# Two scan directions in lockstep, and one layer's modulation multiplied on TensorE

## The chip, the cores and the metric

The kernel runs on one core of one Trainium2 chip. The metric is the device time of one execution in microseconds (us). Engines: PE is TensorE (matrix products), DVE VectorE, ACT ScalarE, POOL GpSimd, SP SyncE, which issues nearly all DMAs here. SBUF holds the operands, PSUM (eight banks) the results of TensorE. An fp32 matmul counts as two instructions in the trace ("passes" below), and each has a weight load (PEld) that overlaps others.

## What is computed

A two-layer backbone over 1024 latent tokens and 256 context tokens of width 1024. Layer 0 mixes tokens by an RWKV-7 recurrence in both directions, layer 1 by a 2-D Fourier transform; each is followed by a squared-ReLU MLP. The part that matters is the recurrence, 16 heads of 64 channels, and the modulation vectors:

```
def step(s, inp):                       # s: one 64 x 64 state per head
    w_t, k_t, v_t, a_t, b_t = inp[:5]
    sa = jnp.einsum('bhvk,bhk->bhv', s, a_t)
    s = s * w_t[:, :, None, :] + sa[..., None] * b_t[:, :, None, :] + v_t[..., None] * k_t[:, :, None, :]
    y = jnp.einsum('bhvk,bhk->bhv', s, inp[5]) if with_out else None
...
for d in range(N_DIRS):                 # d = 1 runs from the end
    yc, s_ctx = _wkv_scan(st_c.get('r'), vh_c, *st_c['dirs'][d], s0, rev)
    yl, _ = _wkv_scan(st_l['r'], vh_l, *st_l['dirs'][d], s_ctx, rev)
...
sh1, sc1, ga1, sh2, sc2, ga2 = jnp.split((silu_c @ mod_w[i] + mod_b[i])[:, None, :], N_MOD, axis=-1)
```

`mod_w[i]` is 1024 x 6144; of layer 0's six vectors the last four (4096 columns) are wanted only behind the scan.

## The kernel before

Three stages follow each other, with some overlap: the projections (`p1_plan`, to about 640 us) write the scan's factors to DRAM, `scan` runs the recurrence (640 to 1315 us), and `rest` does the readout, the MLPs and the Fourier layer.

**The scan.** 1280 tokens are cut into 20 chunks of 64; `scan_step(i)` does chunk i of both directions, d = 0 and d = 1. Within a chunk the recurrence is solved by matrices. For each direction: products of B^T with the factors, `mms` (L945), whose results ScalarE and VectorE mask and copy out (L954 to L966); a transposition of the factor tile bk on TensorE (`trs`, L975) and its copy (L979). `scan_invert` inverts the triangular 32 x 32 blocks of both directions and all heads at once, with VectorE (L1094 to L1138), two products h (L1145) and t (L1156) and a copy tt. None of that needs the state. Then comes what does: VectorE multiplies the old state t by the decay `pcs` into the tile sv, once for each half of the partitions (L1001), GpSimd does the same into st (L1004). The product x (L1019) fills four 32-row quarters of one bank B: two of block row 0 (z = 0) and two of block row 1. For z = 0: ScalarE copies x to xs (L1026), u multiplies by the inverse (L1031), two copies bring u to sv (L1036), o subtracts the coupling from B's other half (L1044); for z = 1: copy, u, two copies. At the end s (L1056) gives the new state and y (L1072, L1076) the output. u and o of one direction use two of the array's four groups of 32 rows. The head halves hh = 0, 1 lie on partitions 0 to 63 and 64 to 127.

**The modulation of layer 0 inside the scan.** The host lays `k_mwt` out transposed: 32 blocks of 128 output columns, the inner dimension along the free axis in two halves. In each of steps 3 to 18 four blocks of 256 KB are loaded into the ring mw (W0 to W3), each released by the step's last x (`after=[self.at]`), and VectorE multiplies each with a row of SiLU(c) and sums it (`mod_part`, L886). `silu_row` makes the row twice, at steps 3 and 11. Layer 1's modulation goes the same way later, beside the first MLP (`modvecs`).

**The order.** `Plan.add` only records an operation: engine (q is SyncE's queue), booked duration, keys read and written, and load (how much of the array the clock is booked to see). `Plan.flex` leaves the engine open. `Plan.emit` then writes out the order of every engine's queue, by booked times alone: always the operation that can start first, and among equals the one with the longest booked path to the end. On the chip each engine runs its queue in that order and waits where an operand is late. In idle time of TensorE the planner may put fill products (L1814) that keep the clock up. PSUM banks and places in SBUF are taken as they are booked free. The scan uses banks 0 to 3 for `mms` and transposes, 4 for h and t, 5 to 7 for x, u, s and y.

Of the kernel before, what the change touches and what calls it, by code (L numbers as in the profile page):

```python
# [13 lines left out]
ALU = mybir.AluOpType  # L14
# [66 lines left out]
class Plan:  # L81
# [245 lines left out]
class Kernel:  # L327
# [449 lines left out]
    def factor(self, kt, low, d, c, k, k_k, kk, kkk, rr):  # L777
# [37 lines left out]
        self.flex_tt(n, bk[:, :ng, 0], gv(ta), p1[:, :ng], ALU.mult, [kta, kp1], [(kbk, 0)])  # L815
# [19 lines left out]
    def scan(self):  # L835
# [10 lines left out]
        for j, hp in enumerate(R["hp"]):  # L846
            plan.add("dve", 0.6, lambda hp=hp: nc.vector.tensor_copy(hp, self.cst[:, 0:32].rearrange("p (e c) -> p e c", e=1).broadcast_to(
                [P, 16, 32])), [self.kcst], [("hp", j)])
        self.state = {}
        for i in range(NCH):  # L850
            self.plan.step = i
            self.scan_step(i)
            if i == 3:
                past = plan.gate([("indt", 0), ("rts", 0), ("rts", 1)])
# [25 lines left out]
    def mod_part(self, layer, j, h, w, kw, after=()):  # L880

        nc = self.nc
        row = (j - 16 if layer == 0 else 32 + j) * P
        src = self.i["k_mwt"][row : row + P, h * 512 : h * 512 + 512]
# [15 lines left out]
    def scan_step(self, i):  # L900
# [3 lines left out]
        R0 = [slice(hh * 64, hh * 64 + 32) for hh in range(2)]  # L904
        R1 = [slice(hh * 64 + 32, hh * 64 + 64) for hh in range(2)]
# [24 lines left out]
        for d in range(2):  # L930
# [5 lines left out]
            for h4 in range(2):  # L936
# [13 lines left out]
                for hh, B in enumerate(BB):  # L950
# [3 lines left out]
                    plan.add("act", 0.38, lambda B=B, hh=hh, ys=ys: nc.scalar.activation(  # L954
                        mab[R0[hh], :, ys].rearrange("p w q t -> p q w t"),
                        B.tile[R0[hh]].rearrange("p (q w t) -> p q w t", q=4, w=4)[:, :, 0:2], AF.Copy, scale=-0.5),
                        [B], [(kM, d, hh, h4, 0)], B)
                    plan.add("act", 0.28, lambda bv=bv, hh=hh, ys=ys: nc.scalar.activation(
                        mab[R1[hh], 0, ys], bv()[R1[hh], :, 32:C], AF.Copy, scale=-0.5),
# [10 lines left out]
            BB = [self.plan.bank(range(4)) for _ in range(2)]  # L970

            def trs(BB=BB, bk=bk):
                for q in range(8):
                    for hh, rs in enumerate(HR):
                        nc.tensor.transpose(BB[hh].tile[:, q * C : (q + 1) * C], bk[rs, q, :], self.ident[rs, rs])  # L975

            plan.add("pe", 1.1, trs, [kb], [*BB, (kt_, 0), (kt_, 1)], load=0.5)
            for hh, B in enumerate(BB):
                plan.add("act", 0.68, lambda B=B, bkt=bkt, hh=hh: nc.scalar.activation(  # L979
                    bkt[:, hh].rearrange("p x t -> p (x t)"), B.tile, AF.Copy, scale=self.sgn[:, hh : hh + 1]),  # L980
                    [B, self.ksgn], [(kt_, hh)], B)
        tt, kT = self.scan_invert(mab, kM)

        for d in range(2):
# [941 lines left out]
```

## Time and profile before

| | us |
|---|---|
| median of 3 runs (lowest, highest) | 3095.93 (3091.98, 3108.24) |
| the profiled execution | 3100.86 |
| its span, first to last instruction | 3099.1 |
| TensorE busy in it | 2905.6 |
| VectorE, ScalarE, GpSimd busy | 1902.2, 998.6, 535.9 |
| mean granted clock of TensorE | 0.93 of full |

Busy times are sums over one profiled execution on the one core. Matmuls are pipelined and their ends are modelled, so a busy TensorE is not one at its peak. [...] In names of tiles the first letter is the stage (a, b projections, s scan, r rest) and the rest the place; ps is PSUM. "Chain of waits" is the chain of work that ended last, followed back from the last instruction; a DMA's piece in it runs from its issue to its landing.

### The profile page before, as it was taken

What the parts mean: (1) busy time and instruction counts of PE and PEld (TensorE: products, weight loads), DVE (VectorE), ACT (ScalarE), POOL (GpSimd) and SP (SyncE); (2) the same over time, 40 slices, a digit from 0 to 9 for tenths busy, and PEclk for the clock granted to TensorE, in tenths of its full rate; (3) what the DMA queues carried; (4) which work ended last, traced back from release to release, by engine and by line L of the source; (5) the groups of instructions that cost most, each with busy time, mean ns of one, the idle gap of its engine ahead of it and who ended that gap; (6) DMA issues with size and microseconds to landing.
All of it is one profiled execution on the core that took longest, in us unless ns stands there. A gap on an engine that the chain in (4) does not pass through costs nothing.

```text
span 3099.1 us, 65486 instructions
## 1 busy us (share of the span) xinstructions
PE 2905.6 (94%) x27884; PEld 2258.6 (73%) x27884; DVE 1902.2 (61%) x3316; ACT 998.6 (32%) x1943; POOL 535.9 (17%) x449
## 2 busy tenths in 40 slices
PE   9999989988878888799999999999899999999998
PEld 5443446477777777789878888888798788888887
DVE  5397785457666666687566556545877544554456
ACT  4363554245444555443211211111322111111121
POOL 2163452201001000111111001100331110111010
PEclk9999999967777877799999999999989999999999
DMA  9266476623344444553132323211031111111111
GB/s 276 86 182 174 136 194 177 160 66 100 107 128 124 134 117 120 158 186 102 58 109 92 96 89 107 70 48 47 8 120 42 52 47 38 55 48 48 41 45 55
DMA packets 297299, 313.03 MB, mean 101 GB/s; under 512 B 81024, under 2 KB 212224, under 8 KB 297008
## 3 DMA queue, kind: packets, MB, share of 16 engines
q1 hardware_dynamic: 295648, 304.01, 33.1%
q8 instruction: 219, 3.59, 0.5%
q0 software_dynamic: 1360, 4.84, 0.5%
q14 instruction: 72, 0.59, 0.1%
HBM read 246.38 MB, written 62.39 MB: 100 GB/s over the span
## 4 chain that ended last, share of the span: by engine, by line
PE 71%; DVE 10%; DMA 6%; issue 3%; ACT 2%; POOL 0%; SPq 0%; DVEq 0%; ACTq 0%; POOLq 0%
PE ps L364 16%; PE ps L366 16%; PE ps L365 16%; PE ps L617 4%; DMA sW<-in_k_mwt_dram 3%; PE ps L620 3%; PE ps L1031 2%; PE ps L945 2%; PE ps L1056 1%; PE ps L1044 1%; PE ps L1019 1%; PE ps L1072 1%; PE ps L1076 1%; DVE bU L456 1%; PE ps L1156 1%
## 5 line engine op out<-in xcount | busy, mean ns | idle before, releaser
L364 PE MATMUL ps<-rU,rU 128*128 128x512 f32 (+3 forms) x2632 | 979.0, 372 | 9.8 <-DVE rX L1509 8.0
L366 PE MATMUL ps<-rU,rU 128*128 128x512 f32 (+3 forms) x2632 | 974.9, 370 | 6.5 <-DVE rU L1239 3.7
L365 PE MATMUL ps<-rU,rU 128*128 128x512 f32 (+3 forms) x2632 | 974.6, 370 | 0.0
L364 PEld LDWEIGHTS ps<-rU,rU 128*128 128x128 f32 x2632 | 500.5, 190 | 105.1 <-DVE rX L1509 9.1
L366 PEld LDWEIGHTS ps<-rU,rU 128*128 128x128 f32 x2632 | 500.6, 190 | 98.0 <-DVE rU L1239 5.2
L365 PEld LDWEIGHTS ps<-rU,rU 128*128 128x128 f32 x2632 | 500.6, 190 | 89.5
L1509 DVE SCALAR_TENSOR_TENSOR rX<-ps,mods,rX 128x512 f32<-128x512 f32 (+1 forms) x528 | 375.6, 730 | 122.3 <-PE ps L366 120.5
L1239 POOL TENSOR_TENSOR rU<-rW,rU 128x512 fp32r<-128x512 f32 x73 | 117.2, 1611 | 1018.8 <-PE ps L366 521.7
L1488 ACT ACTIVATE rS<-ps 128x512 f32<-128x512 f32 x122 | 73.1, 599 | 680.9 <-PE ps L366 680.2
L620 PE MATMUL ps<-bU,bU 128*128 128x512 f32 (+1 forms) x544 | 237.5, 573 | 2.6 <-ACT bS L423 1.9
L423 ACT CAST rU<-rW 128x512 fp32r<-128x512 f32 x160 | 96.3, 616 | 346.8 <-PE ps L366 251.3
L423 DVE CAST rU<-rW 128x512 fp32r<-128x512 f32 x116 | 56.8, 500 | 221.0 <-PE ps L365 210.1
L423 DVE CAST rU<-rS 128x512 fp32r<-128x512 f32 (+1 forms) x99 | 46.9, 479 | 229.5 <-ACT rS L1491 203.4
L1239 DVE TENSOR_TENSOR rU<-rW,rU 128x512 fp32r<-128x512 f32 x201 | 175.5, 893 | 19.7 <-ACT rU L423 19.3
L620 PEld LDWEIGHTS ps<-bU,bU 128*128 128x128 f32 x544 | 100.2, 193 | 109.1 <-issue 98.2
L617 PE MATMUL ps<-bU,bU 128*128 128x512 f32 x304 | 141.7, 607 | 0.0
L945 PE MATMUL ps<-sU,sX 64*128 64x128 f32 (+1 forms) x1280 | 125.5, 353 | 16.8 <-DVE sU L961 7.8
L945 PEld LDWEIGHTS ps<-sU,sX 64*128 64x128 f32 x1280 | 111.9, 255 | 25.2 <-issue 11.7
L961 DVE TENSOR_TENSOR sU<-ps,sW 64x256 f32<-64x256 f32 x160 | 67.5, 422 | 85.7 <-ACT sX L954 44.8
L1239 POOL TENSOR_TENSOR rU<-rS,rU 128x512 fp32r<-128x512 f32 x39 | 60.7, 1559 | 280.8 <-ACT rU L423 125.9
L1036 ACT COPY sU<-ps 32x512 f32<-32x512 f32 x160 | 92.3, 577 | 43.4 <-PE ps L1031 40.2
L617 PEld LDWEIGHTS ps<-bU,bU 128*128 128x128 f32 x304 | 56.6, 192 | 61.6 <-issue 57.8
(268 smaller groups left out, 3899.2 us busy)
## 6 DMA issues: line engine op xcount, KB each, us to landing
rW<-in_mlp_w_dram SPq DMA_DIRECT2D x256, 256.0 KB
rW<-in_k_mwt_dram SPq DMA_DIRECT2D x96, 256.0 KB
sX<-s_bk SPq DMA_DIRECT2D x40, 512.0 KB
s_ar<-bU SPq DMA_DIRECT2D x32, 512.0 KB
sU<-s_ar SPq DMA_DIRECT2D x64, 256.0 KB
sW<-in_k_mwt_dram SPq DMA_DIRECT2D x64, 256.0 KB
bU<-in_rk_wk_dram SPq DMA_DIRECT2D x48, 256.0 KB
bU<-in_rk_wv_dram SPq DMA_DIRECT2D x48, 256.0 KB
```

The costliest lines, as they stand in the source:

```text
L364: nc.tensor.matmul(out, w[0], x[0], start=start, stop=False)
L365: nc.tensor.matmul(out, w[0], x[1], start=False, stop=False)
L366: nc.tensor.matmul(out, w[1], x[0], start=False, stop=stop)
L423: self.nc.scalar.copy(out, src) if e == "act" else self.engines[e].tensor_copy(out, src)
L617: fn = lambda B=B, x=x, w=w, ms=ms, kt=kt: nc.tensor.matmul(B.tile, x[:, ms], w, start=kt == 0, stop=kt == KT - 1)
L620: fn = lambda B=B, x=x, w=w, ms=ms, kt=kt, n=n: nc.tensor.matmul(B.tile[:, :n], w[:, ms], x[:, :n], start=kt == 0, stop=kt == KT - 1)
L945: nc.tensor.matmul(BB[hh].tile[:, j * P : j * P + nr], bk[HR[hh], q, :], L[hh][HR[hh], q, :nr], start=True, stop=True)
L961: plan.add("dve", 0.41, lambda bv=bv, ro=ro, hh=hh, q4=q4, d=d, L=L: nc.vector.tensor_tensor(L[hh][ro, q4, 0:C], bv()[ro, :, 0:C], self.ma ...
L1036: plan.add("act", 0.58, lambda sv=sv, hh=hh, rows=rows, U=U: nc.scalar.copy(sv[rows[hh], hh].rearrange("p q c -> p (q c)"), U.tile[rows[hh ...
L1239: plan.flex({"dve": n / 960 + 0.07, "pool": n / 440 + 0.08}, lambda e: self.engines[e].tensor_tensor(out(1), src(), f32(out(0)), ALU.subtr ...
L1488: plan.flex({"act": 0.53, "dve": 0.6}, lambda e, B=B, s=s: nc.scalar.activation(s.tile[:, :512], B.tile, AF.Relu) if e == "act" else nc.ve ...
L1509: plan.add("dve", n / 960 + 0.12, lambda B=B, m=m, n=n, xs=xs: nc.vector.scalar_tensor_tensor(xs(), B.tile[:, :n], self.mod(layer, 5, m), ...
```

## The change

**Lockstep.** x writes two banks XB, one per block row z, and both directions share them; the copies xs, the products u and o are one call each for both directions, over all four groups of 32 rows (`RZ[z][d][hh]` gives the rows: for d = 1 the two block rows of a head half are swapped). The first stage therefore writes one of d = 1's factor tiles with its halves swapped, and the mask is rolled to match. The copies of u to sv may run on ScalarE or VectorE.

**State.** VectorE multiplies the state by the decay once, into st; two copies (either engine) take it to sv; GpSimd's multiplication goes.

**Order.** The transposes of bk are recorded behind h (direction 0) and behind t (direction 1), h and t in two halves each; y is recorded as two operations; the inversion's long VectorE operations are recorded one by one, and the partial sums lie in another order. Many booked durations and loads are new.

**Modulation.** Layer 0's four vectors come from `k_mw1`, the weight in its natural order. A block is 512 output columns and half of the inner dimension; sixteen blocks, one per step 3 to 18. Four loads of 256 KB (128 rows of 2 KB) as before; then 4 matmuls with a column of SiLU(c), padded to 32 columns, each into its own 32-row quarter of a bank; a copy by ScalarE to me2; four small matmuls with `sel` that add the quarters and turn the row to a column; a VectorE copy of 4 columns into macc. VectorE's products and the two `silu_row` inside the scan go. me2 takes the second place of the ring td.

```
@@ factor
-        self.flex_tt(n, bk[:, :ng, 0], gv(ta), p1[:, :ng], ALU.mult, [kta, kp1], [(kbk, 0)])
+        hv = lambda ap: ap.rearrange("p g (w t) -> p g w t", w=2)
+        self.flex_tt(n, hv(bk[:, :ng, 0])[:, :, flip], hv(gv(ta)), hv(p1[:, :ng]), ALU.mult, [kta, kp1], [(kbk, 0)])
@@ scan
             self.scan_step(i)
-            if i in (3, 11):
-                w, kw = slot("mw")
-                self.silu_row(i // 8, lambda w=w: w, kw, [past, self.at])
             if 3 <= i < 19:
-                for j in range(4):
-                    w, kw = slot("mw")
-                    self.mod_part(0, 16 + (i - 3) % 8 * 4 + j, (i - 3) // 8, lambda w=w: w, kw, [self.at])
-            if i >= 11 and i < 19:
-                self.mod_sum(0, 16 + (i - 11) * 4)
+                self.mod_block(*divmod(i - 3, 2))
+
+    def mod_block(self, j, h):
+        nc, plan, slot = self.nc, self.plan, self.slot
+        W = [slot("mw") for _ in range(4)]
+        for k, (w, kw) in enumerate(W):
+            row = (4 * h + k) * P
+            src = self.i["k_mw1"][row : row + P, j * 512 : j * 512 + 512]
+            plan.add("q", 0.8, lambda w=w, src=src: nc.sync.dma_start(w, src), (), [kw], after=[self.at], hold=0.7)
+        B, V = plan.bank(range(4)), plan.bank(range(4))
+        silc, ksil = self.rings["silc"][0], ("silc", 0)
+        def products():
+            for k, (w, _) in enumerate(W):
+                nc.tensor.matmul(B.tile[32 * k : 32 * k + 32], silc[:, 4 * h + k], w, start=True, stop=True)
+        plan.add("pe", 0.6, products, [kw for _, kw in W] + [ksil], [B], B)
+        e, ke = slot("me2")
+        plan.add("act", 0.58, lambda: nc.scalar.copy(e, B.tile), [B], [ke], B)
+        def turn():
+            for x in range(4):
+                nc.tensor.matmul(V.tile[:, 2 * x : 2 * x + 2], e[:, x * P : (x + 1) * P], self.sel, start=True, stop=True)
+        plan.add("pe", 0.5, turn, [ke], [V], V, load=0.0)
+        at = 16 + 4 * j
+        plan.add("dve", 0.15, lambda: nc.vector.tensor_copy(
+            self.macc[:, 0, h, at : at + 4], V.tile[:, 0:8].rearrange("p (x v) -> p v x", v=2)[:, 0]),
+            [V], [("macc", 0, h, at + x) for x in range(4)], V, after=[self.past])
+        if h:
+            self.mod_sum(0, at)
@@ scan_step
+        RZ = [[[slice(hh * 64 + 32 * (d ^ z), hh * 64 + 32 * (d ^ z) + 32) for hh in range(2)] for d in range(2)] for z in range(2)]
...
+                plan.add("dve", 0.76, lambda d=d, t=t, st=st: nc.vector.tensor_tensor(
+                    st, t, self.pcs[:, d, :, i - 1 : i].broadcast_to([P, 8, C]), ALU.mult), [kt0, *pcs], [ks])
                 for hh in range(2):
-                    rs = HR[hh]
-                    plan.add(("dve", "dve")[hh], 0.78, lambda rs=rs, hh=hh, d=d, t=t, sv=sv: (nc.vector, nc.vector)[hh].tensor_tensor(
-                        sv[rs, hh], t[rs], self.pcs[rs, d, :, i - 1 : i].broadcast_to([64, 8, C]), ALU.mult),
-                        [kt0, *pcs], [(kv, "s0", hh), (kv, "s1", hh)])
-                plan.add("pool", 1.22, lambda d=d, t=t, st=st: nc.gpsimd.tensor_tensor(
-                    st, t, self.pcs[:, d, :, i - 1 : i].broadcast_to([P, 8, C]), ALU.mult), [kt0, *pcs], [ks])
+                    plan.flex({"act": 0.58, "dve": 0.45}, lambda e, hh=hh, sv=sv, st=st: self.copy_on(e, sv[HR[hh], hh], st[HR[hh]]),
+                              [ks], [(kv, "s0", hh), (kv, "s1", hh)])
...
+            self.at = plan.add("pe", 0.6, x_mm, lall + vkeys[d], [(XB[0], d), (XB[1], d)], load=1.0)
+        for z in range(2):
+            xs, kx = slot("xs")
+            plan.flex({"act": 0.58}, lambda e, z=z, xs=xs: self.copy_on(e, xs, XB[z].tile), [(XB[z], 0), (XB[z], 1)], [kx], XB[z])
+            U = self.plan.bank(range(5, 8))
+            def u_mm(xs=xs, U=U, z=z):
+                for q in range(8):
+                    for d, hh in four:
+                        rs = RZ[z][d][hh]
+                        nc.tensor.matmul(U.tile[rs, q * C : (q + 1) * C], tt[rs, d * 8 + q, :], xs[rs, q * C : (q + 1) * C],
+                                         start=True, stop=True)
+            plan.add("pe", 0.65, u_mm, [kx, kT], [U], U, load=0.25)
+            for d, hh in four:
+                rs, sv, kv = RZ[z][d][hh], S[d]["sv"], S[d]["kv"]
+                plan.flex({"act": 0.58, "dve": 0.68}, lambda e, rs=rs, sv=sv, hh=hh, U=U: self.copy_on(
+                    e, sv[rs, hh].rearrange("p q c -> p (q c)"), U.tile[rs]), [U], [(kv, f"s{z}", hh)], U)
+            if z:
+                continue
+            def o_mm():
+                for q in range(8):
+                    for d, hh in four:
+                        nc.tensor.matmul(XB[1].tile[RZ[1][d][hh], q * C : (q + 1) * C], mab[RZ[0][d][hh], 1, d * 8 + q, :],
+                                         S[d]["sv"][RZ[0][d][hh], hh, q, :], start=False, stop=q == 7)
...
@@ scan_invert
+        def turned(d):
+            bk, bkt, kt_ = S[d]["bk"], S[d]["bkt"], S[d]["kt"]
+            def turn():
+                for q in range(8):
+                    for hh, rs in enumerate(HR):
+                        nc.tensor.transpose(TB[d][hh].tile[:, q * C : (q + 1) * C], bk[rs, q, :], self.ident[rs, rs])
+            plan.add("pe", 0.85, turn, [S[d]["kb"]], [*TB[d]], load=0.5)
...
+        for w in range(2):
+            plan.add("pe", 0.7, lambda w=w: h_mm(w), [kxt, *ms], [(H, w)], load=0.15)
...
+        turned(0)
...
+        for w in range(2):
+            plan.add("pe", 0.75, lambda w=w: t_mm(w), [khp, kxd], [(T, w)], load=0.3)
+        turned(1)
```

The numbers in the code are the planner's bookings.

## Rows read from the trace of the kernel before

**Rows 1.** The page: busy time, granted clock in 40 slices.

```profile
PE 2905.6 (94%) x27884; PEld 2258.6 (73%) x27884; DVE 1902.2 (61%) x3316; ACT 998.6 (32%) x1943; POOL 535.9 (17%) x449
...
PEclk9999999967777877799999999999989999999999
```

**Rows 2.** Windows: two stretches of the scan; busy us by engine, clock, DMA.

```profile
core 0: us, PE busy (x) PEld busy (x) DVE busy (x) ACT busy (x) POOL busy (x), PEclk, DMA share, GB/s
643.00:805.00 162.00, 139.40 (x3766) 127.37 (x3767) 109.32 (x234) 81.92 (x187) 14.49 (x16) 0.67 0.27 81
805.00:1264.00 459.00, 377.76 (x11418) 345.34 (x11404) 312.60 (x705) 227.88 (x486) 43.31 (x41) 0.78 0.43 125
```

**Rows 3.** Waits inside the scan: engine, line, waited for, total us, times, longest.

```profile
DVE sW L886 <- DMA sW<-in_k_mwt_dram: 57.1, 12, 10.8
```

**Rows 4.** The chain of waits inside the scan: shares, then its longest pieces.

```profile
by line: DMA sW<-in_k_mwt_dram 13.2%; PE ps L945 10.7%; PE ps L1031 10.6%; issue 7.8%; PE ps L1056 6.4%; PE ps L1044 5.9%; PE ps L1019 5.0%; PE ps L1072 4.3%; PE ps L1076 4.0%; PE ps L1156 3.1%; DMA sU<-s_v 3.1%; PE ps L975 2.8%; PE ps L114
...
861.43 14.58 DMA sW<-in_k_mwt_dram
...
```

**Rows 5.** SyncE's queue in order of time, one block of weights.

```profile
861.43 7.06 SPq L885 DMA_DIRECT2D sW<-in_k_mwt_dram  x4
```

**Rows 6.** VectorE in order of time: what waits for that block.

```profile
876.03 0.69 DVE L886 SCALAR_TENSOR_TENSOR sW<-sW,sF 128x512 f32<-128x512 f32 x1 [10.78 <-DMA sW<-in_k_mwt_dram]
```

**Rows 7.** Groups by line and shape: products u (L1031) and o (L1044).

```profile
L1031 PE MATMUL ps<-sU,sW 32*32 32x64 f32 x1664 | 70.2, 255 | 7.7 <-ACT sU L1026 3.7 <-issue 3.6
...
L1044 PE MATMUL ps<-sU,sX 32*32 32x64 f32 x1280 | 63.4, 260 | 9.3 <-ACT sU L1036 7.2 <-issue 1.3 <-ACT sU L1026 0.8
...
L1031 PE MATMUL ps<-sU,sS 32*32 32x64 f32 x896 | 38.4, 257 | 6.9 <-issue 5.9 <-ACT sU L1026 1.0
```

**Rows 8.** TensorE in order of time: start us, us, instruction, count.

```profile
1057.77 1.08 PE L1031 MATMUL ps<-sU,sW 32*32 32x64 f32 x32 [0.70 <-ACT sU L1026]
...
1089.17 3.21 PE L1031 MATMUL ps<-sU,sS 32*32 32x64 f32 x64 [0.96 <-ACT sU L1026]
...
1097.11 2.08 PE L1156 MATMUL ps<-sU,sU 32*32 32x32 f32 x128
...
1105.43 1.10 PE L1019 MATMUL ps<-sU,sU 128*32 128x64 f32 x64
```

**Rows 9.** Windows around those pieces; behind POOL stands the clock.

```profile
1057.50:1061.00 3.50, 3.23 (x96) 3.01 (x98) 3.29 (x13) 3.14 (x7) 0.00 (x0) 1.00 0.16 35
1089.00:1099.50 10.50, 10.33 (x284) 9.71 (x286) 6.31 (x18) 6.40 (x12) 0.00 (x0) 0.50 0.31 103
1103.00:1106.50 3.50, 3.50 (x150) 3.27 (x147) 2.67 (x4) 0.69 (x2) 1.00 (x2) 1.00 0.41 125
```

**Rows 10.** Groups by line and shape: the state, the weights, the copies.

```profile
L1001 DVE TENSOR_TENSOR sU<-sU,pcs 64x512 f32<-64x512 f32 x76 | 73.9, 972 | 1.8
...
L1004 POOL TENSOR_TENSOR sU<-sU,pcs 128x512 f32<-128x512 f32 x38 | 50.3, 1327 | 229.1 <-DVE sU L1062 105.8 <-PE ps L1072 98.9 <-DVE sS L1123 23.0
...
L886 DVE SCALAR_TENSOR_TENSOR sW<-sW,sF 128x512 f32<-128x512 f32 x64 | 42.6, 681 | 57.2 <-DMA sW<-in_k_mwt_dram 57.1
...
L1123 DVE TENSOR_TENSOR sS<-sS,sS 128x512 f32<-128x512 f32 x20 | 21.8, 1091 | 0.7
...
L1036 ACT COPY sU<-ps 32x512 f32<-32x512 f32 x160 | 92.3, 577 | 43.4 <-PE ps L1031 40.2
...
L1026 ACT COPY sU<-ps 64x512 f32<-64x512 f32 x80 | 46.4, 580 | 45.1 <-PE ps L1019 27.7 <-issue 9.3 <-PE ps L1044 6.9
```

**Rows 11.** Groups by line and shape: copies inside SBUF.

```profile
L423 ACT CAST rU<-rW 128x512 fp32r<-128x512 f32 x160 | 96.3, 616 | 346.8 <-PE ps L366 251.3 <-PE ps L365 62.4 <-DMA rW<-in_rk_wo_dram 12.9
...
L423 DVE CAST rU<-rW 128x512 fp32r<-128x512 f32 x116 | 56.8, 500 | 221.0 <-PE ps L365 210.1 <-DMA rW<-in_rk_wo_dram 5.1 <-PE ps L366 4.2
```

**Rows 12.** Groups in the first 400 us: the modulation that TensorE does already.

```profile
L524 PE MATMUL ps<-aX,aX 128*32 128x256 f32 x128 | 8.6, 385 | 0.2
...
L534 PE MATMUL ps<-sel,aX 128*128 128x2 f32 x32 | 4.5, 247 | 0.0
```

More of the change, by code (lines that the diff above doesn't have):

```diff
@@ L882, in mod_part @@
         nc = self.nc
-        row = (j - 16 if layer == 0 else 32 + j) * P
-        src = self.i["k_mwt"][row : row + P, h * 512 : h * 512 + 512]
+        src = self.i["k_mwt"][j * P : j * P + P, h * 512 : h * 512 + 512]
         self.plan.add("q", 0.8, lambda: nc.sync.dma_start(w(), src), (), [kw], after=after, hold=0.7)
@@ L969, in scan_step @@
                             [B, self.kmask], [(k2, hh, h4)], B)
[L970 to L982, printed above, removed]
+        tt, kT = self.scan_invert(mab, kM, S)
         for d in range(2):
@@ new lines, in scan_step @@
+            kL = E["kL"]
+            lall = [(kL, "a", 0), (kL, "a", 1)] + [(kL, "k", hh, h4) for hh in range(2) for h4 in range(2)]
+            self.at = plan.add("pe", 0.6, x_mm, lall + vkeys[d], [(XB[0], d), (XB[1], d)], load=1.0)
[21 more added lines that the diff above has]
+                                         S[d]["sv"][RZ[0][d][hh], hh, q, :], start=False, stop=q == 7)
+            plan.add("pe", 0.65, o_mm, [(E["kv"], "s0", hh) for E in S for hh in range(2)] + [
+                (kM, d, hh, h4, 0) for d in range(2) for hh in range(2) for h4 in range(2)], [(XB[1], 0), (XB[1], 1)], XB[1], load=0.25)
@@ L1049, in scan_step @@
+        for d in range(2):
+            E = S[d]
+            L, kL, sv, kv, vall = E["L"], E["kL"], E["sv"], E["kv"], vkeys[d]
             if i < NCH - 1:
@@ L1077, in y_mm @@
                                              start=False, stop=q == 7)
-                plan.add("pe", 2.1, y_mm, vall + [E["ks"], (kL, "a", 0), (kL, "a", 1)]
-                         + [(k2, hh, h4) for hh in range(2) for h4 in range(2)], [Y], Y, load=0.85)
+                plan.add("pe", 0.95, r_mm, vall + [E["ks"], (kL, "a", 0), (kL, "a", 1)], [Y], Y, load=0.5)
+                plan.add("pe", 1.05, y_mm, vall + [(k2, hh, h4) for hh in range(2) for h4 in range(2)], [Y], Y, load=1.0)
                 y, ky = slot("y")
@@ L1108, in four @@
                 nc.vector.tensor_reduce(at(x, 16 * t, [(68, 4), (1, t)]), p, AX.X, ALU.add)
-        plan.add("dve", 1.5, four, [km], [kx, kta])
+        plan.add("dve", 0.9, four, [km], [kx, kta])
         def double(n):
@@ L1140, in scan_invert, with h_mm @@
         H, T = self.plan.bank((4,)), self.plan.bank((4,))
-        def h_mm():
-            for y in range(16):
+        HR = [slice(0, 64), slice(64, 128)]
+        TB = [[self.plan.bank(range(4)) for _ in range(2)] for _ in range(2)]
+        def turned(d):
[5 more added lines that the diff above has]
+            plan.add("pe", 0.85, turn, [S[d]["kb"]], [*TB[d]], load=0.5)
+            for hh, B in enumerate(TB[d]):
+                plan.add("act", 0.68, lambda B=B, hh=hh: nc.scalar.activation(
+                    bkt[:, hh].rearrange("p x t -> p (x t)"), B.tile, AF.Copy, scale=self.sgn[:, hh : hh + 1]),
+                    [B, self.ksgn], [(kt_, hh)], B)
+        def h_mm(w):
+            for y in range(8 * w, 8 * w + 8):
                 for q in Q:
                     nc.tensor.matmul(H.tile[q, y * 16 : y * 16 + 16], mab[q, 0, y, :], xt[q, y, 0:16], start=True, stop=True)
-        plan.add("pe", 3.0, h_mm, [kxt, *ms], [H], H, load=0.15)
+        for w in range(2):
+            plan.add("pe", 0.7, lambda w=w: h_mm(w), [kxt, *ms], [(H, w)], load=0.15)
         hp, khp = slot("hp")
@@ L1834, in host_layouts @@
         "k_mw0": a["mod_w"][0][:, : 2 * D],
[L1835 removed]
+        "k_mw1": a["mod_w"][0][:, 2 * D :],
+        "k_mwt": a["mod_w"][1].T,
         "k_ftb": flipped,
```

93 lines of the change are left out of this document (35 added, 58 removed), and 4 rows, old and new, of the table SCAN_RINGS.

## The prediction

> **What bounds the kernel now.** I read the page first: TensorE is busy 94% of the execution, but in the 9th to 17th of its 40 slices the granted clock is 0.6 to 0.8 instead of 0.9 or more [rows 1]. That is the scan, from 640 to 1315 us, and the change touches almost nothing else. So the 94% says little here; the question is what sets the pace of those 675 us, twenty steps of about 33.7 us.
>
> The windows of the scan come next [rows 2]. In its long middle stretch TensorE is busy 377.76 of 459 us (82%) at a clock of 0.78, VectorE 312.6 (68%), ScalarE 227.88 (50%), GpSimd 9%; the DMA engines work 43% of the time. TensorE is the fullest engine, yet idle for 81 us. The waits show one cause: VectorE stands 57.1 us, in 12 waits of up to 10.8 us, for weights of the modulation [rows 3]. The chain of waits makes the same DMA its largest item, 13.2% of 675 = 89 us, in seven long pieces of 10.0 to 14.6 us, and behind it come the small products of TensorE [rows 4]. The queue explains it: SyncE issues four blocks of weights at 861.43, when a product x has released them [rows 5], and the instruction that multiplies them gets going at 876.03, after VectorE has stood 10.78 us [rows 6]. The planner books such a load as landed far earlier, so it has written the instruction into VectorE's order ahead of masks and inversion that TensorE needs. The reader should see two things: TensorE's small products are most of the chain, and a late load blocks whatever engine must consume it in order.
>
> **Products u and o, in lockstep.** Before, each direction has its own u (twice) and o (once), each with two of the array's four 32-row groups at work; afterwards one call does both directions with all four. The instruction count stays: 128 passes of u and 64 of o per step. They now take 70.2 + 38.4 + 63.4 = 172 us of TensorE [rows 7]. On the chain stand 10.6% + 5.9% = 16.5% of 675, or 111 us [rows 4]. Does a pass become twice as cheap? At full clock u takes 1.08 us for 32 passes, 34 ns each, while x, 64 columns too, but with four column groups in turn, takes 1.10 us for 64, 17 ns each [rows 8, 9]. At the lower clock u takes 50 ns a pass (3.21 us for 64), and t, which uses four row groups on half the columns, 16 ns (2.08 us for 128). Half the columns explains at most 50 to 25 ns; the other factor of 1.5 is the four groups. So the ends are a cut by a third (111 x 0.35 = 39 us) and a halving of all the busy time (86 us). I take the halving of what is on the chain, **-56 us**, because x has u's columns and is the nearer row.
>
> [...]
>
> **The state.** Before, each direction's new state is multiplied by the decay twice on VectorE, for halves of sv, 76 x 0.972 = 73.9 us, and once more on GpSimd, 38 x 1.327 us [rows 10]. After, VectorE does it once for all partitions (same 512 elements per partition, so 0.97 us) and two copies go out on ScalarE or VectorE, 0.50 to 0.62 us as the casts of that size [rows 11], which can run side by side. The path to x shrinks per direction from 1.94 to 0.97 + 0.56 = 1.53 us: 0.41 x 38 = **-16 us**. Ends: 0, if the masks are what x waits for, and -26 (3.89 to 0.97 x 2 + 0.56 = 2.5 us per step, x 19), if both directions queue on VectorE. GpSimd's instruction was off the path.
>
> **Modulation off VectorE.** 64 products of 0.681 us go, 42.6 us [rows 10], with two rows of SiLU. On the chain they stood behind the seven long loads, some two and a half each: 7 x 2.5 x 0.68 = **-12 us** (ends 0 and -42.6). The 57.1 us of waiting [rows 3] don't go by themselves. The bytes, the number of loads and their release by x stay the same; TensorE now consumes them, in order. Behind a late product stand the next step's B^T products, x, u and o, and for those all engines wait; ScalarE's copy and VectorE's take-over of the 4 columns stand behind it in their own queues as well. I let the wait move over at its present size: **0 us** (ends -89, what the chain gives the load, and +116, below).
>
> **Modulation on TensorE.** A block is 8 passes of 512 columns in four column groups, and 8 passes of 2 columns to turn it. TensorE does the same in the first stage: 128 passes of 256 columns in 8.6 us, so 16 of them, the same columns as a block, 1.07 us; and 32 turning passes in 4.5 us, so 8 in 1.13 us [rows 12]. Sixteen blocks x 2.2 us = 35 us. On the path I count the share that u and o have there, 111/172 = 65%: **+23 us** (ends 0, in TensorE's idle time, and 46 at the lower clock).
>
> **Edits priced at nothing.** ScalarE loses 40 copies of 0.58 us (xs of both directions in one), gains 16 of that size, and shares the copies to sv with VectorE [rows 10]; it is half idle, so that hides it, and without the cover the copies of sv would cost 0.58 us each. The reductions in the inversion write and read in another order: 20 products of 1.091 us can fall to 0.68 at best, 8 us on VectorE [rows 10], but the inversion hangs on loads and not on the state, so it runs ahead. The transposes issue as many passes from another place in the order; they read only bk, and their result is wanted by the state's product at the step's end, some 30 us later. They also free bk for the load two steps on, so if they come late, that load is next to be late on SyncE. The first stage writes one of its tiles in swapped halves: same elements, nothing.
>
> **The sum.** -56 - 16 - 12 + 23 = -61. The profiled execution took 3100.86 us (span 3099.1); that gives 3040. The median of the runs shown is 4.9 us below the profiled one, so I forecast **3035 us**, with 3000 to 3075 as this case's own range. A step would fall from 33.7 to about 30.7 us.
>
> **Rivals.**
> *The wait disappears (0.20).* If the order puts the products behind enough other work of TensorE, the load has landed by then: -57, 2978 us; with the chain's 89 us, 2946. For it: the products are the least urgent thing that TensorE has, since their result is wanted only after the scan. Against it: VectorE's products were that as well, and waited.
> *TensorE waits at every block (0.13, the other side).* The load needs 10 to 14.6 us from its issue. If each of the 16 blocks stops TensorE for the longest wait seen, 10.8 us, that is 173 us instead of 57: +116, 3151 us. It decides from (57 + 61)/16 = 7.4 us a block. For it: one queue now holds both the products and the recurrence. Against it: of 16 blocks only 12 waited at all, 4.8 us on average.
> *Bare links, or a lower clock (0.15).* In lockstep both directions stand in ScalarE's copies at once, where before one direction's products filled the other's copies. Per step: two xs copies of 0.58 and two rounds of sv copies, two deep, 1.15 us each: 3.5 us, 69 us in twenty steps, if nothing else fills them: 3104 us. For it: TensorE already stands idle 18% of the stretch. Against it: y, the B^T products, transposes and the inversion of the next step are ready work. A clock of 0.67, as the early stretch shows [rows 2], instead of 0.78 would end in the same region.
> *The change doesn't do what it says (0.05).* If only two groups work at a time, for instance because they share a bank, u and o cost what they did: 3035 + 56 = 3091 us. [...]
>
> **The numbers.** The forecast has 0.47, the rivals 0.20, 0.13, 0.15 and 0.05. A measurement of this kernel can tell about 0.5%, 15 us, from no change: faster is below 3080, slower above 3111. Faster: 0.47 + 0.20 and the better third of the bare links, 0.72. Same: the rest of that case and the shared bank, 0.14. Slower: the waiting TensorE and a little of the links, 0.14. The range from 2975 to 3105 leaves out the slower side and the far end of the first rival, about 2 in 10.
>
> **What the changed profile would show.** u and o: half the busy time for the same count of passes, near 86 us in all. The chain of waits in the scan: the weights' DMA still there, released into a TensorE product, with the waits on TensorE near 57 us; 0 would be the first rival, over 118 the second. VectorE's busy time in the scan 50 to 70 us lower, GpSimd's decay gone. Idle TensorE in the scan up by over 50 us with ScalarE's copies as releasers would be the bare links. What would make me wrong most likely is the order: all queues are written out ahead from booked durations, and every duration in the scan is booked anew, so waits that have nothing to do with my terms can come or go; the first stage and the part behind the scan are ordered by the same program and may move by some 10 us.

## The result and the profile after

The changed kernel takes 3076.19 us (median of 5 runs, 3073.98 to 3077.21) against 3096.38 of the kernel before on the same chip: ratio 0.9922, 95% interval [0.9897, 0.9947]. It is faster by 0.8%, some 20 us, a third of the 61 that were forecast. Its profiled execution took 3075.38 us, span 3073.6.

The page of the changed kernel, to be read against [rows 1]; the last line is the queue that brings instructions (packets, MB, share):

```profile
PE 2877.5 (94%) x28296; PEld 2212.1 (72%) x28296; DVE 1832.3 (60%) x3227; ACT 988.7 (32%) x1925; POOL 490.6 (16%) x416
...
PEclk9999999967898889899999999999899999999999
...
q8 instruction: 222, 3.64, 0.5%
```

The clock digits in the scan (9th to 17th) rose. The windows over the stretches of [rows 2], and the whole scan from its first to its last x:

```profile
core 0: us, PE busy (x) PEld busy (x) DVE busy (x) ACT busy (x) POOL busy (x), PEclk, DMA share, GB/s
643.00:805.00 162.00, 133.35 (x4217) 118.08 (x4216) 107.02 (x258) 86.07 (x193) 3.80 (x8) 0.76 0.34 100
805.00:1264.00 459.00, 374.13 (x12014) 324.62 (x12004) 266.57 (x633) 231.25 (x491) 9.54 (x19) 0.87 0.42 127
640.30:1270.30 630.00, 515.71 (x16545) 450.35 (x16544) 376.74 (x899) 319.53 (x689) 13.34 (x27) 0.84 0.40 120
```

and the whole scan of the kernel before, likewise from first to last x:

```profile
643.20:1314.10 670.90, 558.52 (x16364) 510.47 (x16366) 456.12 (x1005) 334.06 (x715) 66.97 (x65) 0.75 0.40 118
```

The scan fell from 670.9 to 630.0 us. TensorE's busy time fell by 42.8 us, VectorE's by 79, GpSimd's by 54, and the clock rose from 0.75 to 0.84. Yet 670.9 - 558.5 = 112 us and 630.0 - 515.7 = 114 us: TensorE stands idle as long as before. The groups by line and shape over the scan (u is L1045, o L1059, the modulation L875 and L883), answering [rows 7, 10, 12]:

```profile
L1059 PE MATMUL ps<-sU,sX 32*32 32x64 f32 x1280 | 39.4, 246 | 14.8 <-ACT sU L423 6.9 <-DVE sU L423 4.4 <-issue 2.9
...
L1045 PE MATMUL ps<-sU,sW 32*32 32x64 f32 x1664 | 33.3, 232 | 4.0 <-issue 4.0
...
L875 PE MATMUL ps<-sW,sS 128*32 128x512 f32 x128 | 23.1, 660 | 5.7 <-DMA sW<-in_k_mw_dram 3.1 <-ACT sX L985 1.6 <-DVE sU L993 0.8
L883 PE MATMUL ps<-sel,sS 128*128 128x2 f32 x128 | 19.8, 276 | 1.0 <-DVE sU L993 1.0
L1045 PE MATMUL ps<-sU,sS 32*32 32x64 f32 x896 | 18.8, 239 | 2.1 <-issue 1.8 <-ACT sU L423 0.3
```

u and o went from 172.0 to 33.3 + 18.8 + 39.4 = 91.5 us. The modulation costs 23.1 + 19.8 = 42.9. Waits for its weights, answering [rows 3]:

```profile
PEld ps L875 <- DMA sW<-in_k_mw_dram: 6.4, 7, 3.6
...
PE ps L875 <- DMA sW<-in_k_mw_dram: 3.1, 2, 2.7
```

Of 57.1 us there remain 9.5. So the products became cheaper, the clock higher, and the wait went away; what keeps TensorE idle now? In TensorE's order of time, the bracket at the end of a line is the idle time before it and its releaser, and "issue" means that nothing the profile shows was waited for:

```profile
936.95 0.63 PE L1030 MATMUL ps<-sU,sU 128*32 128x64 f32 x10 [3.01 <-issue]
937.51 1.98 PE L1096 MATMUL ps<-sU,sU 128*64 128x64 f32 x32
939.42 2.08 PE L972 MATMUL ps<-sU,sX 64*128 64x128 f32 x16
941.43 1.63 PE L1197 MATMUL ps<-sU,sU 32*32 32x32 f32 x128
942.99 1.14 PE L1030 MATMUL ps<-sU,sU 128*32 128x64 f32 x64
944.06 0.40 PE L1173 MATMUL ps<-ident,sX 64*128 64x64 f32 x5
945.42 1.07 PE L1173 MATMUL ps<-ident,sX 64*128 64x64 f32 x27 [0.96 <-issue]
...
1109.02 0.80 PE L1173 MATMUL ps<-ident,sX 64*128 64x64 f32 x11 [1.25 <-issue]
1109.75 1.81 PE L1197 MATMUL ps<-sU,sU 32*32 32x32 f32 x117
1112.49 0.42 PE L1197 MATMUL ps<-sU,sU 32*32 32x32 f32 x11 [0.93 <-issue]
```

Count the matmuls (each a row of the trace, a pass) from one pause to the next. From 1109.02 to 1112.49 there are 11 + 117 = 128; from 936.95 to 945.42, 10 + 32 + 16 + 128 + 64 + 5 = 255. The pauses fall in the middle of a product. With its weight load a matmul is two instructions (the page counts 28,296 of each), so 128 pairs are 256 instructions; the second stretch has 255 pairs and two semaphore instructions, 512 in all. The 222 packets of the instruction queue would make 222 x 256 = 56,832 instructions, and TensorE ran 2 x 28,296 = 56,592, or 56,864 with its 272 semaphore instructions (3.64 MB / 222 = 16.4 KB a packet).

The packed trace says more than the views shown. Number all of TensorE's instructions in order: in the changed kernel's scan 53 of its pauses, 76.6 us, stand at the 194th or 195th place of a block of 256, and each of them ends 1.1 to 1.7 us after a packet of the instruction queue has landed, while its other 58 idle pieces end 0.1 to 10 us after one. In the kernel before, 43 pauses, 63.0 us, stand there or one place on, and 41 of them end so. From this place and these packets I read the pauses as TensorE waiting for its next block of instructions. In either scan no two packets start less than 3.2 us apart (3.26 the least before, 3.32 after); why, no run here shows.

Summed over the scan, pauses with "issue" were 61.5 us before (40 of them) and are 75.9 us now (52): 14 us of what the cheaper products and the missing waits gave went there, and the pauses are now two thirds of TensorE's idle time. The other loss is behind the scan: from its last y (1333.5 before, 1291.4 after) to the readout's last addition (1478.1, 1450.5) it took 144.6 us and takes 159.1.

### The profile page after: what moved, and what is told of

It reads as the page before. It is cut to its first block, busy times and chain, and to the rows that moved or that the text cites. A ratio compares the mean times of both kernels' runs of the same rounds, so it can differ in the third digit from the quotient of the medians.

```text
span 3073.6 us, 66068 instructions
## 1 busy us (share of the span) xinstructions
PE 2877.5 (94%) x28296; PEld 2212.1 (72%) x28296; DVE 1832.3 (60%) x3227; ACT 988.7 (32%) x1925; POOL 490.6 (16%) x416
## 3 DMA queue, kind: packets, MB, share of 16 engines
q8 instruction: 222, 3.64, 0.5%
## 4 chain that ended last, share of the span: by engine, by line
PE 50%; DVE 3%; issue 1%; ACT 0%; POOL 0%; DMA 0%; DVEq 0%; ACTq 0%; POOLq 0%
PE ps L364 16%; PE ps L366 16%; PE ps L365 16%; DVE rU L1282 1%; PE ps L1857 0%; DVE rU L423 0%; DVE rS L1651 0%; PE ps L1448 0%; PE ps L1459 0%; DVE rS L1659 0%; DVE rX L1838 0%; DVE rU L1483 0%; DVE rU L1666 0%; DVE rS L1478 0%; PE ps L1375 0%
## 5 line engine op out<-in xcount | busy, mean ns | idle before, releaser
L620 PEld LDWEIGHTS ps<-bU,bU 128*128 128x128 f32 x544 | 99.5, 191 | 108.3 <-issue 97.1
L972 PEld LDWEIGHTS ps<-sU,sX 64*128 64x128 f32 x1280 | 106.5, 240 | 23.1 <-ACT bW L423 8.1
L423 ACT COPY sU<-ps 32x512 f32<-32x512 f32 (+1 forms) x153 | 88.5, 579 | 105.1 <-PE ps L1030 37.4
L433 POOL TENSOR_SCALAR sU<-sS,sS 128x256 f32<-128x256 f32 x25 | 11.8, 479 | 573.1 <-DVE sS L1147 495.1
```

What stands on the lines that cost most here:

```text
L423: self.nc.scalar.copy(out, src) if e == "act" else self.engines[e].tensor_copy(out, src)
L433: self.nc.gpsimd.tensor_scalar(out, src, scale, 0.0, ALU.mult, ALU.add)
L620: fn = lambda B=B, x=x, w=w, ms=ms, kt=kt, n=n: nc.tensor.matmul(B.tile[:, :n], w[:, ms], x[:, :n], start=kt == 0, stop=kt == KT - 1)
L972: nc.tensor.matmul(BB[hh].tile[:, j * P : j * P + nr], bk[HR[hh], q, :], L[hh][HR[hh], q, :nr], start=True, stop=True)
```

## The experiments

The table gives each run's median, its ratio to the kernel before on its chip, and from its trace: scan (first to last x), TensorE's busy time, matmuls, idle time with the part that nothing shown explains ("issue"), and the stretch from the last y to the readout's last addition. Idle times are sums of the brackets in TensorE's order of time.

| run | us | ratio [95%] | scan | busy | matmuls | idle, issue | stretch |
|---|---|---|---|---|---|---|---|
| before | 3096.4 | 1 | 670.9 | 558.5 | 16364 | 111.6, 61.5 | 144.6 |
| after | 3076.2 | 0.9922 [0.9897, 0.9947] | 630.0 | 515.7 | 16545 | 113.2, 75.9 | 159.1 |
| e1 lockstep only | 3063.6 | 0.9878 [0.9858, 0.9898] | 624.0 | 502.7 | 16541 | 119.7, 73.2 | 158.4 |
| e2 modulation only | 3126.0 | 1.0074 [1.0054, 1.0094] | 645.2 | 542.6 | 16271 | 101.6, 65.6 | 189.0 |
| e3 after, wide | 3002.0 | 0.9679 [0.9652, 0.9706] | 553.5 | 490.1 | 12801 | 62.9, 14.9 | 156.0 |
| e4 more narrow | 3145.4 | 1.0138 [1.0117, 1.0159] | 698.6 | 552.5 | 19104 | 144.8, 115.1 | 158.5 |
| e5 more wide | 3095.6 | 0.9981 [0.9965, 0.9998] | 643.2 | 530.9 | 17184 | 111.2, 75.8 | 159.1 |
| e6 before, wide | 3060.5 | 0.9880 [0.9858, 0.9903] | 626.5 | 525.9 | 12525 | 99.6, 6.3 | 144.7 |
| e7 e1, modulation earlier | 3051.3 | 0.9853 [0.9821, 0.9885] | 615.6 | 488.1 | 16539 | 126.1, 75.3 | 148.2 |
| e8 e1, old state path | 3073.3 | 0.9916 [0.9897, 0.9935] | 631.4 | 504.0 | 16519 | 126.0, 85.9 | 152.8 |
| e9 e1, wide | 2993.6 | 0.9659 [0.9634, 0.9684] | 552.0 | 476.3 | 12699 | 74.7, 19.6 | 158.6 |
| e10 after, earlier | 3081.1 | 0.9941 [0.9919, 0.9963] | 635.0 | 520.1 | 16730 | 113.5, 77.7 | 157.3 |
| e11 e1, no fills in scan | 3041.1 | 0.9815 [0.9775, 0.9856] | 613.6 | 477.3 | 16321 | 135.4, 89.3 | 148.1 |
| e12 e7, no fills in scan | 3075.3 | 0.9918 [0.9890, 0.9946] | 615.1 | 476.5 | 16077 | 137.7, 81.2 | 164.8 |

**One half of the change at a time (e1, e2).** e1 is the changed kernel with the modulation back on VectorE, transposed weights and rows of SiLU(c) as before:

```
...
             if 3 <= i < 19:
-                self.mod_block(*divmod(i - 3, 2))
+                for j in range(4):
+                    w, kw = slot("mw")
+                    self.mod_part(0, 16 + (i - 3) % 8 * 4 + j, (i - 3) // 8, lambda w=w: w, kw, [self.at])
...
```

> The changed kernel with layer 0's modulation back on VectorE as before (transposed weights, SiLU rows): the lockstep alone. Supply theory: TensorE pauses every so many instructions while its next block of instructions arrives (75.9 us of pauses in the changed scan, 61.5 before, without a releaser in the trace); u and o get 80 us cheaper, but the count of instructions stays, so the pauses stay near 70 us, and VectorE's wait for weights returns with 30 to 60 us: 3060 to 3095 us. Array theory (the forecast's own sum: only array time on the chain counts): -56 - 16 = 3024 us.

e2 is the kernel before with `mod_block` alone, with one addition: each block's products wait until the block before has left its bank.

> The kernel before with only the modulation on TensorE (same loads; each block's products wait for the block before to have left its bank). The forecast's terms: +23 - 12, the wait moving to TensorE: 3107 us. Rival: the wait disappears, as the changed kernel's 9.5 us on TensorE suggest: 57 to 89 us less, with 23 more: 3030 to 3065 us. Supply theory: 256 instruction pairs more in all are two blocks of 129, so the pauses stay near 62 us.

The lockstep alone is faster than the whole change, by 12.5 us between the medians; the two intervals only touch, but e9 against e3 (8.4 us, overlapping intervals) and e7 against e10 (30 us) point the same way. Its time and its pauses (73.2 us) are what the supply theory expected. The modulation alone makes the kernel slower than either number expected for it, though the wait on VectorE is gone and the scan 26 us shorter: the order put 12 of its 16 blocks behind 1200 us, beside the readout, whose stretch grew by 44. How much of that comes from the added wait between blocks is not shown. The 129 pairs of its expectation are 128 in the traces: from one pause to the next block's, 255 to 257 instructions. The wait for weights shrinks in the lockstep without any move, to 14.3 us in 6 waits (30 to 60 had been expected):

```profile
DVE sW L921 <- DMA sW<-in_k_mwt_dram: 14.3, 6, 7.1
```

**Fewer and more matmuls (e3, e4, e5).** Theory: the number of instructions sets the pace. Rival: the array's own time does. e3 replaces the inverse's two products, h and t, by a quarter as many passes of 256 columns each, where h had 16 and t 32; each pass then uses one of four weights, so part of the computation is changed. h is shown, t goes the same way; the planner's bookings stay, and the other engines run as many instructions as before (DVE 899, ACT 689, POOL 27 in the scan):

```
-            for y in range(8 * w, 8 * w + 8):
+            for y in (8 * w, 8 * w + 4):
                 for q in Q:
-                    nc.tensor.matmul(H.tile[q, y * 16 : y * 16 + 16], mab[q, 0, y, :], xt[q, y, 0:16], start=True, stop=True)
+                    nc.tensor.matmul(H.tile[q, 0:256], mab[q, 0, y, :], xt[q, :, 0:16], start=True, stop=True)
```

> The changed kernel with h and t of the inversion in a quarter as many passes of 256 columns: about the same array time, 192 of some 830 pairs a step fewer (3840 of 16545 in the scan). Part of the computation changes: h and t multiply only every fourth block by several. Supply theory: the pauses fall from 76 to 35 to 45 us and the time to 3035 to 3050 us. Array theory: no change, 3070 to 3080 us.

e4 issues the product h a second time, into the free half of its bank, in its 128 narrow matmuls a step; e5 issues it in 32 wide ones of 256 columns (`if y % 4 == 0`), which is four times as many columns in a quarter as many matmuls.

> The changed kernel with h's 128 narrow passes issued a second time into the free half of their bank: 128 pairs a step more (2560 in the scan, 20 blocks). Supply theory: pauses up by 25 to 50 us on top of the array time, 3120 to 3160 us. Array theory: 20 x 1.2 to 1.8 us of array time, 65 to 80% of it on the path: 3090 to 3105 us.

> The full change with the first stage of the inverse's products issued a second time into the free half of its bank, in 32 products of 256 columns a step instead of 128 of 16 columns: the counterpart of the run with 128 narrow products more (3145 us, where the full change is at 3076). The array's own time for it is about the same: 32 x 256 columns in four row groups, some 1.5 to 2 us a step. Supply theory: 32 more pairs a step are 5 blocks of 128 instead of 20, so the pauses that nothing shown explains stay near 80 us (narrow: 115) and the time is 3090 to 3110. Array theory (the narrow run was slower only because TensorE had 37 us more to do in the scan): 3125 to 3150, as the narrow one.

e3's scan, and e4's and e5's:

```profile
641.90:1195.40 553.50, 490.10 (x12801) 390.99 (x12800) 375.74 (x899) 318.54 (x689) 13.35 (x27) 0.91 0.44 135
```

```profile
640.80:1339.40 698.60, 552.52 (x19104) 481.77 (x19104) 379.12 (x902) 319.23 (x689) 13.54 (x27) 0.81 0.36 109
```

```profile
640.60:1283.80 643.20, 530.88 (x17184) 452.25 (x17184) 377.23 (x901) 320.56 (x689) 13.43 (x27) 0.88 0.39 118
```

3744 matmuls fewer take 61.0 us of pauses and 25.6 of busy time away, 74 us in all; 2559 more add 39.2 of pauses and 36.8 of busy time, 69 us. e3 gained more than the supply theory had expected (3035 to 3050 us, 35 to 45 us of pauses). The instruction queue brings 30 packets fewer in e3 (192), 20 more in e4 (242) and 5 more in e5 (227), and the edits take 3840 matmuls out and put 2560 and 640 in: 128 matmuls are one packet. Four times the columns in 32 wide matmuls a step cost 19 us instead of 69, and the pauses don't move (75.8). So the pauses go with the count of instructions. The control isn't perfect: busy time rose by 15 us in e5 (0.76 a step, where 1.5 to 2 had been expected) and by 37 in e4, so some 22 of the 50 us between them are array time, the rest pauses.

**The supply eased in both kernels (e6, e9).** This asks where the 61 us went. e6 is e3's edit in the kernel before, e9 the same in e1.

> The kernel before with the inverse's two products in a quarter as many passes of 256 columns (part of the computation is changed: each pass uses one of four weights). The full change in this form takes 3002 us. Supply theory: with the supply eased in both kernels, the array time that the row groups save (80 us busy in the narrow form) reaches the end: this run is 55 to 80 us above the full change's wide form, 3057 to 3082, and only 15 to 40 us under its own narrow form (3096 to 3100). Rival (the links of the step in lockstep are longer, and this ate the saving): the gap stays what it is between the narrow forms, 20 to 25 us: 3022 to 3027.

> The lockstep alone (modulation on VectorE) with the inverse's two products in a quarter as many passes (part of the computation is changed: each pass uses one of four weights). The full change in that form takes 3002 us; in the narrow form the lockstep alone is 12 us under the full change. Theory 1 (the modulation on TensorE costs its own array time and its links, supply or not): this run is again 5 to 15 us under the full change's wide form, 2987 to 2997. Theory 2 (taking the modulation and its weights' wait off VectorE is worth what was forecast, and the supply hid it): this run is 15 to 40 us above, 3017 to 3042.

The scan of e6, then that of e9:

```profile
647.00:1273.50 626.50, 525.88 (x12525) 442.09 (x12526) 454.90 (x1003) 332.78 (x715) 65.63 (x65) 0.85 0.43 125
```

```profile
645.10:1197.10 552.00, 476.28 (x12699) 391.88 (x12702) 403.04 (x999) 324.49 (x698) 15.84 (x25) 0.91 0.45 138
```

With the supply eased, the change gives 3060.5 - 3002.0 = 58.5 us where it gave 20 in its own form. Both savings now arrive: busy time falls by 36 us and idle time by 37. And the lockstep alone gives 3060.5 - 2993.6 = 67 us, against 37 in the narrow form. The modulation on TensorE costs 8 us here too (the intervals overlap), so the supply hid no gain of it as large as the 15 to 40 us of Theory 2. In the kernel before, other waits took up most of the pauses that went: its idle time other than pauses rose from 50.1 to 93.3 us, that of the changed kernel from 37.3 to 48.0. So the supply was the limit in the changed kernel far more than in the one before.

**The state's path (e8).** In e1, the old path: two VectorE multiplications per direction into sv, one on GpSimd.

> The lockstep with the modulation on VectorE, and with the state's path of the kernel before: two VectorE multiplications of 64 rows into the tile that the products read, and one of 128 rows on GpSimd, instead of one multiplication and two copies. The prediction's term for this path was -16 us. If it reaches the end, this run is 10 to 20 us above the lockstep alone: 3074 to 3084. If the step's end is set by TensorE and its supply: within 5 us of it, 3059 to 3069.

9.6 us between the medians (12 by the ratios, each to its own chip, and 3.5 between the profiled spans), for a term of -16; the intervals overlap a little. VectorE's busy time in the scan goes from 401 to 441.

**The stretch behind the scan (e7, e10, e13, e14).** It is 153 to 159 us in the kernels with the lockstep up to here, 145 in those without it (e2 apart). e7 and e10 move the modulation two steps earlier (`if 1 <= i < 17`) in e1 and in the full change, so that its places in SBUF come free for the readout's loads.

> The lockstep with the modulation on VectorE, its weights' loads and multiplications two steps earlier (steps 1 to 16 instead of 3 to 18). Theory that the stretch behind the scan grew because the readout's first loads wait for the tiles that the last modulation weights leave: these loads come some 60 us before the scan's end instead of 35 to 50, the stretch from the last y to the readout's last addition falls from 158 to 140 to 148, and the time to 3048 to 3056. Rival (the stretch is the readout's own work, which has only become visible): 3060 to 3068, as without it.

> The full change with its modulation blocks two steps earlier (steps 1 to 16 instead of 3 to 18). The same two steps took the lockstep with the modulation on VectorE from 3064 to 3051 us, and the stretch from the scan's last y to the readout's last addition from 158 to 148. If the tiles of the last weights hold up the readout here too, the stretch falls from 159 to 145 to 150 and the time to 3062 to 3069. If not: 3072 to 3080.

e7 did what was expected (but for 0.2 us of the stretch), e10 did not. Count the readout's loads that SyncE issues before the scan's last x: 20 in the kernel before, e6, e7 and e11 (below), whose stretches are 145 to 148 us; 15 in e8 (153); 9 to 12 in the changed kernel, e1, e3, e4, e5 and e9 (156 to 159). But e10 issues 26 and e12 (below) 20, and theirs are 157 and 165. So early loads go with a short stretch and are not enough for it. Its windows, and in it the groups of one of the readout's three product lines, its transposes and the fills; before:

```profile
1333.50:1478.10 144.60, 133.37 (x1139) 129.78 (x1136) 115.67 (x201) 49.23 (x90) 27.01 (x20) 0.96 0.42 131
```

```profile
L364 PE MATMUL ps<-rU,rU 128*128 128x256 f32 (+1 forms) x281 | 81.4, 290 | 0.1
...
L1332 PE MATMUL ps<-ident,rS 128*128 128x128 f32 x96 | 14.8, 301 | 9.2 <-DVE rS L1288 5.0 <-DVE rX L1378 3.0 <-DVE rS L1291 1.2
L1814 PE MATMUL ps<-ident 128*128 128x128 f32 x122 | 14.5, 277 | 1.7 <-DVE rS L1352 1.7
```

and after, windows and groups:

```profile
1291.40:1450.50 159.10, 147.14 (x1236) 143.44 (x1233) 126.58 (x221) 56.91 (x105) 32.40 (x24) 0.96 0.43 137
```

```profile
L364 PE MATMUL ps<-rU,rU 128*128 128x256 f32 x289 | 85.1, 294 | 0.0
...
L1857 PE MATMUL ps<-ident 128*128 128x128 f32 x182 | 21.1, 276 | 0.9 <-DVE rS L1395 0.9
L1375 PE MATMUL ps<-ident,rS 128*128 128x128 f32 x112 | 16.5, 291 | 8.5 <-DVE rS L1331 3.6 <-DVE rX L1421 3.2 <-DVE rS L1334 1.7
```

TensorE is busy 92% in both, and 147.1 - 133.4 = 13.8 of the 14.5 us are busy time: 24 matmuls of the readout's products (8 in each of three lines) and 16 transposes, which the kernel before had done when the last y came, and 60 more fill products (21.1 against 14.5 us). e13 and e14 leave the fills of the readout out, in the kernel after and in that before:

```
-            if e == "pe" and blank:
+            if e == "pe" and blank and op["step"] != "r":
```

> The full change without the planner's fill products in the readout. In the stretch from the scan's last y to the readout's last addition (159.1 us) TensorE is busy 147.1 us, 21.1 of them with fills. Theory A (fills displace products): the stretch falls to 140 to 149 and the time to 3057 to 3067. Theory B (the stretch is longer because less of the readout's own work stood ahead of the last y; fills only stand where TensorE would wait): it stays at 155 to 162 and the time at 3070 to 3080.

> The kernel before without the fill products in the readout: 14.5 us of TensorE's 133.4 in a stretch of 144.6 us. Theory A: the stretch falls to 131 to 138, so the difference to the full change shrinks from 14 to about 8, and the time to 3083 to 3092. Theory B: it stays at 142 to 147, time within 8 us of the kernel before.

Neither theory: both became slower, 3090.4 (0.9978 [0.9960, 0.9996]) and 3122.0 us (1.0071 [1.0040, 1.0102]), the stretches 172.9 and 165.3. Here the fills pay:

```profile
1288.30:1461.20 172.90, 135.92 (x1056) 130.37 (x1052) 125.06 (x219) 57.62 (x107) 33.73 (x24) 0.86 0.40 127
```

The granted clock of the stretch fell from 0.96 to 0.86 in both, and the idle time grew (from 12 to 37 us in the changed kernel). So leaving the fills out brings none of the 14 us back. But the difference between the two kernels is 172.9 - 165.3 = 7.6 us without them instead of 14.5, near the 8 of Theory A, so the 60 more fills may carry up to half of it. What remains is the readout's own work, of which less stood ahead of the last y. Why the order put it later is open.

**Fills in the scan (e11, e12).** The same edit for the scan's operations, in e1 and in e7.

> The lockstep with the modulation on VectorE, without the planner's fill products in the scan. In that kernel they are 222 products with as many weight loads, 34 us of TensorE's busy time of 503, put where the planner books TensorE as idle. Supply theory: 222 pairs fewer are 1.7 blocks of 128, and a fill that stands between late instructions delays them: 3050 to 3062 (3064 with them). Clock theory: without the fills the granted clock in the scan (0.83) falls towards the 0.75 of the kernel before, the small products become slower, and the time is 3070 to 3095.

> The lockstep with the modulation on VectorE and two steps earlier (3051 us with 218 fills, 36 us busy, in the scan), without the fills in the scan. Supply theory: 3038 to 3050. Clock theory: 3057 to 3082. The stretch behind the scan's last y should stay near 148 us if the earlier loads set it, and go back to near 158 if it hangs on the order as a whole.

e11 is the fastest kernel that computes the whole: 60 us under the kernel before on its chip. e11 lies below both forecasts, e12 in the clock theory's range; but in the scan the clock hardly moves (0.83 in e1 and in e11; 0.85 in e7, 0.83 in e12), the scan is 10 us shorter in e11 and the same in e12. Of the 25 us of busy time that go in e11's scan, 16 come back as idle time (119.7 to 135.4). But e12 loses at both ends: its first x comes 7 us later, its last y 27.7 us behind its last x instead of 16.0, its stretch takes 164.8. The same work in another written order thus differs by 34 us between two near kernels; single steps of 10 us in this family are not to be read as effects of an edit.

## Why the prediction was off

**The step that failed is the sum.** It took TensorE's chain for what ends the scan and let -56, -16, -12 and +23 through to the end one for one, with TensorE's idle time set only by waits that the profile names. The idle time that it does not name was in the traces of before (61.5 us with "issue", and in the chain's shares 7.8% [rows 4]), and the prediction passed it over: it priced the wait for instructions at nothing, and it grew to 75.9 us. Cheaper matmuls run into it more often, in 52 pauses where there were 40: where one pause follows another one block on, 3.5 to 5.8 us lie between their ends (3.47 from 1109.02 to 1112.49), while t's 128 matmuls alone took 1.63 us (941.43), and u's 64 that took 2.2 us at full clock now take 1.1. With the supply eased the same sum is nearly right:

| term | forecast | narrow, as built | supply eased |
|---|---|---|---|
| u, o and the state (lockstep) | -56 - 16 = -72 | -37 (e1) | -67 (e9 - e6) |
| the modulation | -12 + 0 + 23 = +11 | +12.5 (after - e1) | +8 (e3 - e9) |
| sum | -61 | -20 | -58.5 (e3 - e6) |

The narrow column doesn't add up exactly, since its runs were taken against different runs of the kernel before. That the last column comes so near is in part luck. The scan itself fell by 73.0 us (626.5 to 553.5), more than the sum, and the stretch behind it took 11.3 back (144.7 to 156.0). And the lockstep cut VectorE's wait for weights by 50 us, which the sum had left as it was (e6, e9):

```profile
DVE sW L886 <- DMA sW<-in_k_mwt_dram: 66.6, 14, 8.4
```

```profile
DVE sW L921 <- DMA sW<-in_k_mwt_dram: 16.6, 7, 7.4
```

**u and o: right.** 91.5 us, forecast near 86. 64 passes over four row groups in one bank take 1.10 us at full clock (946.42 in TensorE's order of time; the clock from 946.4 to 947.6 is 1.00), as x's 64 do [rows 8], where u's 32 took 1.08 (clock 1.00 too [rows 9]): the rival that the groups don't overlap is refuted. Four row tiles wrote one bank at twice the rate of two (17 ns a pass against 34).

```profile
946.42 1.10 PE L1045 MATMUL ps<-sU,sS 32*32 32x64 f32 x64
```

**State: a right sign, too large.** 3.5 to 12 us for 16, no more than the written order alone can move; the multiplications left VectorE's queue, which was not what x waited for every time: in the kernel before, TensorE stood 4 times, 2.6 us in all, before one of x's forty calls for them, and 6 times, 8.4 us, with "issue". The one multiplication that is left takes 0.694 us (L1014), where 0.97 had been estimated.

**Modulation: the right net, by luck.** The sum of +11 was measured as +8 to +12.5, though the products cost 42.9 us of TensorE's busy time where 35 were forecast. But the wait did not move over: it went to 9.5 us on TensorE, and to 14.3 in the lockstep without the move. The first rival thus saw its event (most of the waits vanish) without its price: TensorE's idle time in the scan stayed at 113 us, with 14 us more of it in pauses.

**The second rival is refuted** (9.5 us of waits, decided from 118), **bare links** too: the idle time didn't grow, and the clock rose.

**Not in the sum:** the 14 us behind the scan. The text had named "some 10 us" of reordering there; it came on the side of the loss, and its cause is open.

## What to carry to other kernels

Before array time is converted to time, look for idle pieces that the trace puts down to nothing and count all of the engine's instructions between them, semaphore instructions too. Here, where all 52 of them (39 of 40 before) stood at nearly the same place of a block, 3744 matmuls fewer (e3) gave 74 us, and 42.8 us less of busy time with 181 matmuls more gave 20, so try whether cutting instructions pays more than cutting their duration. Test this by wider and fewer instructions in place of some, in the kernel before as well as after: the gap between the two wide forms (58.5 us here, 20 between the narrow ones) tells what the edit is worth by itself. And make each half of a double change alone: here one half carried all of the gain, and the other seems to have cost a third of it.

## What the runs showed of the hardware

In this scan small matmuls are held up by the supply of their instructions: 53 pauses of 0.2 to 3.9 us at the 194th or 195th place of a block of 256 instructions, 76.6 us of 630. The size of a block is read from three counts: 128 matmuls with their weight loads from one pause to the next, 222 packets of 16.4 KB for TensorE's 56,864 instructions, and 30 packets fewer, 20 and 5 more for 3840 matmuls fewer, 2560 and 640 more (e3 to e5). Fewer matmuls took 61.0 us of pauses away (e3), more narrow ones added 39.2 (e4). The trace names no releaser for the pauses; that they are late blocks is read from their place in the block and from the packet that lands 1.1 to 1.7 us before each ends.

In the stretch behind the scan the granted clock was 0.96 with the fill products and 0.86 without them, in both kernels, and both were slower without (by 14 and 26 us). In the scan it was 0.83 either way in e1 and e11, 0.85 with and 0.83 without them in e7 and e12. Whether they cost time there is open: without them one kernel was 23 us faster, the other 24 us slower.
